# Key-key and query-key products of a DeltaNet layer: fp32 products of 128 columns against split products of 256 columns on shared stationary keys

## The chip, the core and the metric

The kernel runs on one core of a Trainium2 chip. The metric is the device time of one execution in microseconds (us); lower is better. Besides whole runs there is one profiled execution, whose trace gives each instruction's engine, start and duration. TensorE appears there as PE (matmuls) and PEld (loads of the stationary operand), VectorE as DVE, ScalarE as ACT, GpSimd as POOL, and the queue that issues all DMAs of this kernel as SP.

## What is computed

One layer of a diffusion backbone over 128 context and 2048 latent tokens (17 tiles of 128 tokens), in fp32: a modulated RMSNorm, an input projection, a convolution over three tokens with SiLU on queries, keys and values, a bidirectional gated DeltaNet beside a gated MLP, an output projection, and a feed-forward block. The change concerns the two matrices that the DeltaNet needs within each chunk:

```python
q = l2norm(q.reshape(B, T, H_A, DK)); k = l2norm(k.reshape(B, T, H_A, DK))
# per chunk, H_A = 4 heads of DK = 128 features
a_mat = where(strict, einsum('bnhcd,bnhsd->bnhcs', k_beta, k) * decay, 0.0)
qk = einsum('bnhcd,bnhsd->bnhcs', q, k) * decay
```

The kernel forms the raw products of keys with keys and of keys with queries per tile of 128 tokens and per head, and applies beta, decay and scale later. That is 17 x 4 = 68 tile-heads, two 128x128 products each.

## The kernel before

The work runs in phases. The first phase, which ends near 435 us of the profile, makes the projection of queries, keys and values, the convolution, and the products above, and writes all of them to DRAM scratch. Later phases (the scan over chunks, the gated MLP, the output projection, the feed-forward block) load them from there.

**Start.** Four half vectors of the modulation are computed first, by `mod_load` and `mod_sum`: eight loads of 128x512 weights each (`raw`, 256 KB) and eight fp32 matmuls that keep the two condition columns stationary and move 512 columns. I call them m0 to m3. Each result, a row of 2x512 named `first`, is transposed by `mod_out` into the scale `a1` or shift `b1`. Three tiles of x (`x`, 512 KB each) and ten border rows (`xh`) are loaded, normalized and transposed, and `column(k)` makes from them the two halves `kH` and `kL` of the k-th feature tile of the first block and stores them (`hH_d`, `hL_d`). m0 and m1 and the x tiles are all that column 0 needs; the later columns need m2 and m3 too.

**Split products.** A product of fp32 precision is formed by `mm3` from operands that are split into a rounded high part and a low remainder (type `fp32r`): high x high, high x low, low x high, three matmuls into one accumulator.

**Blocks.** Five blocks of three token tiles and one of two (`BLOCKS`) are worked one after the other. Per block there are twelve feature tiles (`feature_tile`: four heads each of keys, queries and values), each a projection of 24 matmuls of 386 to 388 columns (258 in the last block) into a bank of the pool `pj` (three banks), read by `convolve` on ACT and DVE. Four further steps of a tile are placed as side work between the projections of later tiles: `to_tokens` (transposes on PE, norms on ACT, results `kn` and `tk`), `to_features` (transposes back, copied by DVE to `kTt`, the keys with features on partitions), and `products`, once per block and head, 24 calls in all.

**Products before.** `products` makes, for each of two destinations `kk_d` and `qk_d`, one fp32 matmul of 128 columns per token tile, with a slice of `kTt` as stationary operand for the first destination and moving slices of `kTt` or of the query tile `x2` (line 625; on the chip each shows as two records). ACT copies each destination's bank of the pool `pt` (three banks) to `ev` (line 628), and SP stores it (line 629). `ev` shares four buffers, tag `tk`, with `kn` and `tk`.

**What sets the order.** A scheduler that works on the whole program puts the instructions of each engine into one fixed order; every engine and the SP queue then run that order strictly, waiting at an instruction until what it needs is there. Tiles come from pools whose buffers are handed out in turn; the pool `wp` has 49 buffers of 128x512 (`raw`, weights and their halves), and a load into a buffer waits for the last reader of what lay there.

Of the kernel before, what the change touches and what calls it, by code (L numbers as in the profile page):

```python
# [8 lines left out]
F32 = mybir.dt.float32  # L9
F32R = mybir.dt.float32r  # L10
# [3 lines left out]
ALU = mybir.AluOpType  # L14
# [3 lines left out]
P = 128  # L18
# [46 lines left out]
def hybrid_step(  # L65
# [7 lines left out]
    V, A, G, T = nc.vector, nc.scalar, nc.gpsimd, nc.tensor  # L73
    load = nc.sync.dma_start
    store = nc.sync.dma_start
# [10 lines left out]
    def f32(ap):  # L86
        return ap.bitcast(F32)
# [12 lines left out]
    kk_d = dp.tile([NT, P, H, P], F32, name="kk_d")  # L100
# [127 lines left out]
    def w512(name, dt=F32):  # L228
        return wp.tile([P, 512], dt, tag="w", name=name)
# [65 lines left out]
    with ExitStack() as ph:  # L295
# [52 lines left out]
        def mod_sum(raws, psum):  # L348

            pm = psum()  # L350
            for k in range(KT):
                T.matmul(pm[0:2, :], scond[:, k, :], raws[k], start=k == 0, stop=k == KT - 1)
            row = pf.tile([2, 512], F32, tag="first", name="first", bufs=2)
            A.copy(row, pm[0:2, :])
            return row

# [187 lines left out]
        def feature_tile(blk, bi, gi, h):  # L544

            hH, hL, ncol, segs = blk
            tiles = BLOCKS[bi]
            nt = len(tiles)
            n = nt * P
            c0 = tiles[0] * P  # L550
            j = gi * 4 + h
            u = {}

            def project(k):
                if k == 0:
                    u["ps"] = (pt if bi == 0 and j == 6 else pj)()
                wh, wl = W1[gi][k]
                mm3(u["ps"][:, :ncol], [(wh[:, h * P : (h + 1) * P], wl[:, h * P : (h + 1) * P],
                                         hH[k][:, :ncol], hL[k][:, :ncol])], first=k == 0, last=k == KT - 1)
                if k == KT - 1:  # L560
                    convolve()

            def convolve():
                ps = u["ps"]
                cv = pf.tile([P, 384], F32, tag="cv", name="cv", bufs=2)
                u["x2"] = x2 = pf.tile([P, 384], F32, tag="x2", name="x2", bufs=4)
                for s, o, m, _ in segs:
                    A.activation(cv[:, o : o + m], ps[:, s : s + m], AF.Copy, scale=convw[:, 1, j : j + 1])  # L568
                for s, o, m, _ in segs:
                    for w, sh in ((0, -1), (2, 1)):  # L570
                        V.scalar_tensor_tensor(out=cv[:, o : o + m], in0=ps[:, s + sh : s + sh + m],  # L571
                                               scalar=convw[:, w, j : j + 1], in1=cv[:, o : o + m],
                                               op0=ALU.mult, op1=ALU.add)
                A.activation(x2[:, :n], cv[:, :n], AF.Tanh, scale=0.5)
                V.scalar_tensor_tensor(out=x2[:, :n], in0=x2[:, :n], scalar=1.0, in1=cv[:, :n], op0=ALU.add,
                                       op1=ALU.mult)
                if gi == 0:
                    store(out=by_tiles(qT_d[:, :, h, :], slice(tiles[0], tiles[0] + nt)),
                          in_=x2[:, :n].rearrange("p (a d) -> p a d", d=P))

            def to_tokens():
                pq = pt()
                for i in range(nt):
                    T.transpose(pq[:, i * P : (i + 1) * P], u["x2"][:, i * P : (i + 1) * P], ident)  # L584
                rows = slice(c0, c0 + n)
                if gi == 2:
                    tk = pf.tile([P, 3, P], F32, tag="tk", name="tk", bufs=4)
                    A.copy(tk[:, :nt, :], pq[:, :n].rearrange("p (a b) -> p a b", b=P))
                    store(out=vt_d[rows, h * P : (h + 1) * P].rearrange("(a p) d -> p a d", p=P),
                          in_=tk[:, :nt, :])  # L590
                    return
                junk = p1.tile([P, P], F32, tag="junk2", name="junk2", bufs=1)
                if gi == 0:
                    for i, t in enumerate(tiles):
                        A.activation(junk, pq[:, i * P : (i + 1) * P], AF.Square,
                                     accum_out=ssq[:, t, h : h + 1])
                    return
                ss = smp.tile([P, 3], F32, tag="ss3", name="ss3")
                rk = smp.tile([P, 3], F32, tag="rk", name="rk")
                for i in range(nt):  # L600
                    A.activation(junk, pq[:, i * P : (i + 1) * P], AF.Square, accum_out=ss[:, i : i + 1])  # L601
                rsqrt_cols(rk[:, :nt], ss[:, :nt], nt, 1.0, 4 * EPS)
                u["kn"] = kn = pf.tile([P, 3, P], F32, tag="tk", name="kn", bufs=4)
                for i in range(nt):
                    A.activation(kn[:, i, :], pq[:, i * P : (i + 1) * P], AF.Copy, scale=rk[:, i : i + 1])
                store(out=kt_d[rows, h * P : (h + 1) * P].rearrange("(a p) d -> p a d", p=P),
                      in_=kn[:, :nt, :])

            def to_features():

                u["kTt"] = kTt = pf.tile([P, 384], F32, tag="kTt", name="kTt", bufs=3)
                pk = pt()
                for i in range(nt):
                    T.transpose(pk[:, i * P : (i + 1) * P], u["kn"][:, i, :], ident)
                V.tensor_copy(kTt[:, :n], pk[:, :n])
                store(out=by_tiles(kT_d[:, :, h, :], slice(tiles[0], tiles[0] + nt)),
                      in_=kTt[:, :n].rearrange("p (a d) -> p a d", d=P))

            def products(q):

                kTt = u["kTt"]
                for dst, rhs in ((kk_d, kTt), (qk_d, q["x2"])):
                    ps = pt()
                    for i in range(nt):
                        T.matmul(ps[:, i * P : (i + 1) * P], kTt[:, i * P : (i + 1) * P],  # L625
                                 rhs[:, i * P : (i + 1) * P], start=True, stop=True)
                    ev = pf.tile([P, 3, P], F32, tag="tk", name="ev", bufs=4)
                    A.copy(ev[:, :nt, :], ps[:, : nt * P].rearrange("p (a b) -> p a b", b=P))
                    store(out=dst[tiles[0] : tiles[0] + nt, :, h, :].rearrange("a p d -> p a d"),
                          in_=ev[:, :nt, :])  # L630

            u["main"] = [lambda k=k: project(k) for k in range(KT)]
            u["to_tokens"] = to_tokens
            u["to_features"], u["products"] = to_features, products
            return u
# [1435 lines left out]
```

## Time and profile before

| | |
|---|---|
| three runs | 2574.28, 2577.04, 2578.62 us, median 2577.04 us |
| profiled execution | 2580.59 us, its span 2578.7 us |
| PE busy in the span | 2539.4 us (98%), 15268 matmul records |
| DVE, ACT, POOL busy | 1836.7, 1259.7, 234.2 us (71%, 49%, 9%) |
| DMA | 588.66 MB, mean 228 GB/s |
| mean granted clock of TensorE | 0.997 |

The profile's page lists each engine's busy time over the span, then the span in slices, the DMA queues, the chain of work that ended last, and the costliest groups of instructions. A matmul's record lasts longer than the time for which it holds up the next one, since matmuls overlap in the pipeline: what a matmul costs in a full stream is the distance from its start to the next start. Some matmul records are missing from the later phases; in the first phase they are complete.

### The profile page before, as it was taken

The page shows a single profiled execution, that of the slowest core. Times are in us where ns is not written, and L with a number is a line of the kernel's source. Part 1 is how long each engine was busy: PE and PEld are TensorE (multiplying, and loading weights), DVE is VectorE, ACT ScalarE, POOL GpSimd, SP SyncE. Part 2 cuts the span into 40 slices and gives each one's busy share as a digit, 9 for nine tenths or more (in the row PEclk, how much of TensorE's full clock was granted, in tenths as well). Part 3 has the DMA queues.
Part 4 walks back from the last instruction along what each step waited for, and adds up shares of the span by engine and source line. Part 5 has one row for each costly group of instructions (what it writes and reads, how often), then busy time and mean ns, then how long its engine had stood idle before and what let it go on. Part 6 is the DMA issues. An engine that isn't in the chain of part 4 may idle for free.

```text
span 2578.7 us, 44496 instructions
## 1 busy us (share of the span) xinstructions
PE 2539.4 (98%) x15268; PEld 2139.2 (83%) x15268; DVE 1836.7 (71%) x3790; ACT 1259.7 (49%) x3119; POOL 234.2 (9%) x448
## 2 busy tenths in 40 slices
PE   9999999999999999999999999999999999999998
PEld 5999999788888787778888888888888888888887
DVE  5867757776677878886677876777675557685875
ACT  4755556555555667764355543544442433243442
POOL 3112212111111111210000000000000000000000
PEclk9999999999999999999999999999999999999999
DMA  8967737644454657885768789666579979786683
GB/s 293 307 209 216 209 111 256 225 158 153 145 156 159 214 165 243 277 274 176 281 204 257 231 270 358 194 181 188 148 248 370 331 273 330 259 259 205 221 264 113
DMA packets 503912, 588.66 MB, mean 228 GB/s; under 512 B 36148, under 2 KB 298588, under 8 KB 500102
## 3 DMA queue, kind: packets, MB, share of 16 engines
q1 hardware_dynamic: 503686, 585.82, 69.6%
q8 instruction: 120, 1.97, 0.3%
q14 instruction: 106, 0.87, 0.1%
HBM read 406.01 MB, written 179.67 MB: 227 GB/s over the span
## 4 chain that ended last, share of the span: by engine, by line
PE 89%; DMA 5%; DVE 4%; ACT 1%; issue 1%; POOL 0%; SPq 0%; POOLq 0%; DVEq 0%; ACTq 0%
PE f L241 17%; PE f L242 17%; PE f L243 17%; PE pj L241 7%; PE pj L243 7%; PE pj L242 7%; PE pd L1010 5%; PE pm L241 1%; PE pm L243 1%; PE pm L242 1%; DMA raw<-in_w_mod_dram 1%; PE pt L625 1%; PE pt L584 1%; PE pd L1093 1%; DMA hop_d<-opL 1%
## 5 line engine op out<-in xcount | busy, mean ns | idle before, releaser
L241 PE MATMUL f<-hop,zH 128*128 128x512 f32 (+1 forms) x976 | 376.2, 386 | 1.2 <-ACT zH L1531 1.2
L242 PE MATMUL f<-hop,zH 128*128 128x512 f32 (+1 forms) x976 | 376.1, 386 | 0.0
L243 PE MATMUL f<-hop,zL 128*128 128x512 f32 (+1 forms) x976 | 376.1, 386 | 0.0
L241 PE MATMUL f<-hop,wH 128*128 128x512 f32 x896 | 349.7, 391 | 0.6 <-ACT p L1604 0.6
L242 PE MATMUL f<-hop,wH 128*128 128x512 f32 x896 | 348.7, 389 | 0.0
L243 PE MATMUL f<-hop,wL 128*128 128x512 f32 x896 | 347.5, 389 | 0.0
L1531 ACT CAST zH<-zraw 128x512 fp32r<-128x512 f32 x240 | 146.9, 620 | 302.4 <-DMA zraw<-s_d 93.6
L241 PEld LDWEIGHTS f<-hop,zH 128*128 128x128 f32 x976 | 183.3, 188 | 38.6 <-ACT zH L1531 1.6
L243 PEld LDWEIGHTS f<-hop,zL 128*128 128x128 f32 x976 | 183.3, 188 | 37.3 <-DVE zL L1525 0.4
L242 PEld LDWEIGHTS f<-hop,zH 128*128 128x128 f32 x976 | 183.3, 188 | 36.9 <-issue 0.2
L1525 DVE TENSOR_TENSOR zL<-zraw,zH 128x512 fp32r<-128x512 f32 x240 | 163.2, 687 | 66.5 <-ACT zH L1531 54.0
L241 PEld LDWEIGHTS f<-hop,wH 128*128 128x128 f32 x896 | 168.2, 188 | 36.5 <-ACT p L1604 1.7
L243 PEld LDWEIGHTS f<-hop,wL 128*128 128x128 f32 x896 | 168.2, 188 | 35.3
L242 PEld LDWEIGHTS f<-hop,wH 128*128 128x128 f32 x896 | 168.3, 188 | 34.5
L241 PE MATMUL pj<-kH,wH 128*128 128x386 f32 (+2 forms) x568 | 190.5, 338 | 1.3 <-ACT junk L601 1.1
L243 PE MATMUL pj<-kH,wL 128*128 128x386 f32 (+2 forms) x568 | 189.7, 335 | 0.0
L242 PE MATMUL pj<-kL,wH 128*128 128x386 f32 (+2 forms) x568 | 189.5, 335 | 0.1
L184 POOL TENSOR_TENSOR r<-rsq,nhalf 128x1 f32<-128x1 f32 (+1 forms) x37 | 25.7, 694 | 1409.0 <-DVE rsq L183 1409.0
L571 DVE SCALAR_TENSOR_TENSOR cv<-pj,vec,cv 128x384 f32<-128x384 f32 (+2 forms) x164 | 87.0, 539 | 53.4 <-ACT cv L568 52.0
L1531 ACT CAST wH<-s 128x512 fp32r<-128x512 f32 x96 | 59.4, 621 | 124.6 <-DVE s L1525 118.3
L241 PEld LDWEIGHTS pj<-kH,wH 128*128 128x128 f32 x568 | 107.1, 189 | 4.4 <-issue 2.4
L202 DVE TENSOR_TENSOR wL<-raw,wH 128x512 fp32r<-128x512 f32 x120 | 81.7, 688 | 40.0 <-ACT wH L201 36.6
(418 smaller groups left out, 5806.9 us busy)
## 6 DMA issues: line engine op xcount, KB each, us to landing
zraw<-z_d SPq DMA_DIRECT2D x212, 256.0 KB
raw<-in_w_ff_dram SPq DMA_DIRECT2D x192, 256.0 KB
hop<-hop_d SPq DMA_DIRECT2D x28, 1024.0 KB
z_d<-c SPq DMA_DIRECT2D x96, 256.0 KB
zraw<-s_d SPq DMA_DIRECT2D x96, 256.0 KB
raw<-in_w_mod_dram SPq DMA_DIRECT2D x80, 256.0 KB
r<-in_w_ff_dram SPq DMA_DIRECT2D x80, 256.0 KB
s_d<-s SPq DMA_DIRECT2D x64, 256.0 KB
```

What stands on the lines that cost most here:

```text
L184: G.tensor_tensor(out=out, in0=t[:np_, :n], in1=nhalf[:np_, :n], op=ALU.pow)
L202: V.tensor_tensor(out=lo, in0=raw, in1=f32(h), op=ALU.subtract)
L241: T.matmul(ps, lh, rh, start=first and i == 0, stop=False, skip_group_check=more)
L242: T.matmul(ps, lh, rl, start=False, stop=False, skip_group_check=more)
L243: T.matmul(ps, ll, rh, start=False, stop=last and i == n - 1, skip_group_check=more)
L571: V.scalar_tensor_tensor(out=cv[:, o : o + m], in0=ps[:, s + sh : s + sh + m], scalar=convw[:, w, j : j + 1], in1=cv[:, o : o + m], op0=AL ...
L584: T.transpose(pq[:, i * P : (i + 1) * P], u["x2"][:, i * P : (i + 1) * P], ident)
L625: T.matmul(ps[:, i * P : (i + 1) * P], kTt[:, i * P : (i + 1) * P], rhs[:, i * P : (i + 1) * P], start=True, stop=True)
L1010: T.matmul(p[:, h, :], lhs[:, h, :], rhs[:, h, :], start=True, stop=True)
L1093: T.matmul(py[:, h], u["X"][:, h, :], pm[:, h], start=True, stop=True)
L1525: V.tensor_tensor(out=out, in0=a, in1=b, op=op)
L1531: A.copy(h, src)
```

## The change

`products` is written anew. ACT rounds keys and queries into one tile `kqH` (high parts, keys in half 0 and queries in half 1), DVE subtracts to get `kqL` (low parts). For each token tile three matmuls follow, as in `mm3`, and each moves keys and queries of the tile together, 2 x 128 = 256 columns, on the stationary keys. A bank of `pt` takes two token tiles, so a call needs two banks for three tiles; ACT copies the first with 512 and the second with 256 columns per partition into `ev`, which now holds both destinations, and SP stores the two halves. `kqH`, `kqL` and `ev` have one buffer each (`kqH` takes over the space of `xh`). To make room, the shared buffers of tag `tk` go from four to three, and the rows `first` move from a pool of their own (two buffers) into `wp`.

```diff
-            row = pf.tile([2, 512], F32, tag="first", name="first", bufs=2)
+            row = w512("first")[0:2, :]
...
-                    tk = pf.tile([P, 3, P], F32, tag="tk", name="tk", bufs=4)
+                    tk = pf.tile([P, 3, P], F32, tag="tk", name="tk", bufs=3)
...
-                kTt = u["kTt"]
-                for dst, rhs in ((kk_d, kTt), (qk_d, q["x2"])):
+                hi = pf.tile([P, 2, 384], F32R, tag="xh", name="kqH", bufs=1)
+                lo = pf.tile([P, 2, 384], F32R, tag="kqL", name="kqL", bufs=1)
+                for w, x in enumerate((u["kTt"], q["x2"])):
+                    A.copy(hi[:, w, :n], x[:, :n])
+                    V.tensor_tensor(out=lo[:, w, :n], in0=x[:, :n], in1=f32(hi)[:, w, :n], op=ALU.subtract)
+                ev = pf.tile([P, 2, 3, P], F32, tag="ev", name="ev", bufs=1)
+                for i0 in range(0, nt, 2):
+                    m = min(2, nt - i0)
                     ps = pt()
-                    for i in range(nt):
-                        T.matmul(ps[:, i * P : (i + 1) * P], kTt[:, i * P : (i + 1) * P],
-                                 rhs[:, i * P : (i + 1) * P], start=True, stop=True)
-                    ev = pf.tile([P, 3, P], F32, tag="tk", name="ev", bufs=4)
-                    A.copy(ev[:, :nt, :], ps[:, : nt * P].rearrange("p (a b) -> p a b", b=P))
-                    store(out=dst[tiles[0] : tiles[0] + nt, :, h, :].rearrange("a p d -> p a d"),
-                          in_=ev[:, :nt, :])
+                    for i in range(m):
+                        c = slice((i0 + i) * P, (i0 + i + 1) * P)
+                        out = ps[:, i * 256 : i * 256 + 256].rearrange("p (w d) -> p w d", w=2)
+                        for j, (st_, mv) in enumerate(((hi, hi), (hi, lo), (lo, hi))):
+                            T.matmul(out, st_[:, 0, c], mv[:, :, c], start=j == 0, stop=j == 2)
+                    A.copy(ev[:, :, i0 : i0 + m, :].rearrange("p w a d -> p a w d"),
+                           ps[:, : m * 256].rearrange("p (a w d) -> p a w d", a=m, w=2))
+                for w, dst in enumerate((kk_d, qk_d)):
+                    store(out=dst[tiles[0] : tiles[0] + nt, :, h, :].rearrange("a p d -> p a d"), in_=ev[:, w, :nt, :])
```

In the changed program lines 624 (`kqH`), 625 (`kqL`), 634 (matmuls), 635 (copies to `ev`) and 638 (stores) take the place of 625, 628 and 629. Over the kernel the counts move so: 136 fp32 matmuls of 128 columns go, 204 split matmuls of 256 columns come; 48 copies on ACT go and 44 come, with 48 roundings; 48 subtractions on DVE come; the 48 stores stay. Nothing else changes in number.

The scheduler gives all engines another order in the first phase. Past it, the order of every engine is that of before, apart from buffer numbers and line numbers (on PE the last 14775 of 17290 instructions).

The SP queue at the start of the program, before, from the eleventh load on (`raw` from `w_mod` with eight or sixteen loads are m0 to m3; line 377 loads weights of a fifth, later part of the modulation; 747, 670 and 671 load small constants):

```order
L190 DMA raw<-in_w_mod_dram 128x512 x16
L411 DMA xh<-in_x_sample_dram 2x1024 x5
L424 DMA x<-in_x_prompt_dram 128x1024
L424 DMA x<-in_x_sample_dram 128x1024 x2
L190 DMA raw<-in_w_mod_dram 128x512 x8
L190 DMA raw<-in_w_in_dram 128x512 x4
L772 DMA abr<-in_w_ab_dram 128x128
L377 DMA raw<-in_w_mod_dram 128x512 x2
```

m0 and two rows of small constants stand ahead; so m0, m1 and m2 come first, then x, then m3 and the first four projection weights. The same place in the changed program:

```order
L190 DMA raw<-in_w_mod_dram 128x512 x8
L411 DMA xh<-in_x_sample_dram 2x1024 x5
L424 DMA x<-in_x_prompt_dram 128x1024
L424 DMA x<-in_x_sample_dram 128x1024 x2
L780 DMA abr<-in_w_ab_dram 128x128
L377 DMA raw<-in_w_mod_dram 128x512 x2
L390 DMA mrow<-in_b_mod_dram 2x512
L755 DMA wsT<-in_w_spatialT_dram 128x512
L678 DMA alog<-in_a_log_dram 128x8
L679 DMA dtb<-in_dt_bias_dram 128x8
L190 DMA raw<-in_w_mod_dram 128x512 x8
L377 DMA raw<-in_w_mod_dram 128x512 x2
```

m2 now stands behind x and seven other loads. What follows there:

```order
L534 DMA hH_d<-kH 128x128
L534 DMA hL_d<-kL 128x128
L534 DMA hH_d<-kH 128x2x128
L534 DMA hL_d<-kL 128x2x128
L190 DMA raw<-in_w_mod_dram 128x512 x8
L190 DMA raw<-in_w_in_dram 128x512 x20
```

m3 and the projection weights have moved behind the four stores of column 0, which wait for DVE.

ACT in the fourth block (token tiles 9 to 11), before, around two calls of `products` (568 and 574 belong to `convolve`, 528 to `column`, 588 to `to_tokens`):

```order
L628 COPY ev<-pt 128x384 x2
L568 ACTIVATE cv<-pj,vec 128x384
L588 COPY tk<-pt 128x384
L628 COPY ev<-pt 128x384 x2
L574 ACTIVATE x_4012<-cv 128x384
```

Each call has two copies there. The same engine and block in the changed program:

```order
L635 COPY ev<-pt 128x2x2x128
L635 COPY ev<-pt 128x2x128
L624 CAST kqH<-kTt 128x384
L624 CAST kqH<-x_3958 128x384
L574 ACTIVATE x_4211<-cv 128x384
L568 ACTIVATE cv<-pj,vec 128x384
L528 ACTIVATE kH<-full,b_197 128x384 x2
L588 COPY tk<-pt 128x384
L635 COPY ev<-pt 128x2x2x128
L635 COPY ev<-pt 128x2x128
```

Behind the two copies of one call now stand the two roundings of the next call, and the next copies into the single `ev` wait for the stores of the call before.

PE at another call of the same block (the second of its four), in the changed program:

```order
L634 MATMUL pt<-kqH 128x256 x2
L241 MATMUL pj<-kH,wH 128x386
L242 MATMUL pj<-kL,wH 128x386
L243 MATMUL pj<-kH,wL 128x386
L241 MATMUL pj<-kH,wH 128x386
L634 MATMUL pt<-kqL,kqH 128x256
L634 MATMUL pt<-kqH,kqL 128x256
L634 MATMUL pt<-kqH 128x256
L634 MATMUL pt<-kqL,kqH 128x256
```

Two high x high products go ahead, four projection matmuls stand between, and the products with low parts follow, where before the fp32 matmuls of a destination stood together.

More of the change, by code (lines that the diff above doesn't have):

```diff
@@ L602, in to_tokens @@
                 rsqrt_cols(rk[:, :nt], ss[:, :nt], nt, 1.0, 4 * EPS)
-                u["kn"] = kn = pf.tile([P, 3, P], F32, tag="tk", name="kn", bufs=4)
+                u["kn"] = kn = pf.tile([P, 3, P], F32, tag="tk", name="kn", bufs=3)
                 for i in range(nt):
```

## The prediction

> **What bounds the kernel now.** I read the page first: the busy times and the chain that ended last.
>
> ```profile
> span 2578.7 us, 44496 instructions
> PE 2539.4 (98%) x15268; PEld 2139.2 (83%) x15268; DVE 1836.7 (71%) x3790; ACT 1259.7 (49%) x3119; POOL 234.2 (9%) x448
> PE 89%; DMA 5%; DVE 4%; ACT 1%; issue 1%; POOL 0%; SPq 0%; POOLq 0%; DVEq 0%; ACTq 0%
> ```
>
> PE carries 89% of the chain. Next the windows of the first phase (columns: PE, PEld, DVE, ACT, POOL busy, granted clock, DMA share, GB/s):
>
> ```profile
> 0.00:50.00 50.00, 47.81 (x186) 22.83 (x187) 24.80 (x97) 21.73 (x42) 23.81 (x104) 1.00 0.93 323
> 60.00:440.00 380.00, 377.18 (x2448) 363.66 (x2447) 265.07 (x573) 222.14 (x682) 73.71 (x174) 1.00 0.71 213
> ```
>
> From 60 to 440 us PE is busy for 99%, DVE for 70%, ACT for 58%. So there a shorter PE stream shortens the run, and work on the other two is free while no matmul waits for it. In the first 50 us the DMA share is 0.93: the start is near a bound by loads.
>
> **The products on PE.** The line's groups and one call, instruction by instruction:
>
> ```profile
> L625 PE MATMUL pt<-kTt x136: 270/275/377, 92.0 to 427.8; 128*128 128x128 f32 x136
> L625 PE MATMUL pt<-x,kTt x136: 270/275/276, 93.8 to 429.4; 128*128 128x128 f32 x136
> ...
> 154.31 0.34 PE L242 MATMUL pj<-kL,wH 128*128 128x386 f32 x1
> 154.49 0.83 PE L625 MATMUL pt<-kTt 128*128 128x128 f32 x6
> 155.07 0.43 PE L243 MATMUL pj<-kH,wL 128*128 128x386 f32 x1
> 155.34 0.34 PE L241 MATMUL pj<-kH,wH 128*128 128x386 f32 x1
> 155.51 0.34 PE L242 MATMUL pj<-kL,wH 128*128 128x386 f32 x1
> ```
>
> A matmul of 386 columns lasts 0.34 us but is followed after 0.17 to 0.18. The six records of one destination take from 154.49 to 155.07, 0.58 us, and the projection matmul behind them holds 0.27 instead of 0.18: together 0.67. Twenty calls of three tiles have two such groups (26.8 us), four calls of two tiles have two thirds of that (3.6): 30.4 us in all.
>
> The new matmuls are 204 of 256 columns. Nearest in size are those of the gates:
>
> ```profile
> 385.34 0.28 PE L646 MATMUL pj<-kL,abW 128*128 128x258 f32 x1
> 385.46 0.28 PE L645 MATMUL pj<-kH,abW 128*128 128x258 f32 x1
> 385.58 0.28 PE L646 MATMUL pj<-kL,abW 128*128 128x258 f32 x1
> ```
>
> They start 0.12 apart: 204 x 0.12 = 24.5. Lower bound: per column as at 386 (0.175 / 386 x 256 = 0.116), 23.7. Upper bound: the whole 0.175 of the 386-column matmul, 35.7, which would turn the gain into a loss of 5.3; the moving operand here is two strips of 128 columns, which no row shows, but at 258 columns the row is nearest and I take it. **Term A: 24.5 - 30.4 = -5.9.** So the product of two split triples on shared keys is not three times cheaper, only a fifth.
>
> **What ACT and DVE get.** Groups by shape, from 60 to 440 us (count, busy, mean ns, idle before):
>
> ```profile
> L201 ACT CAST wH<-raw 128x512 fp32r<-128x512 f32 x33 | 20.1, 641 | 7.4 <-DMA raw<-in_w_in_dram 4.2 <-DMA raw<-in_w_mod_dram 3.2
> L628 ACT COPY ev<-pt 128x384 f32<-128x384 f32 x40 | 18.7, 481 | 15.5 <-PE pt L625 14.4 <-DMA kk_d<-ev 0.8 <-DMA qk_d<-ev 0.2
> L628 ACT COPY ev<-pt 128x256 f32<-128x256 f32 x8 | 2.9, 372 | 0.5 <-PE pt L625 0.4
> L202 DVE TENSOR_TENSOR wL<-raw,wH 128x512 fp32r<-128x512 f32 x32 | 21.3, 681 | 4.0 <-ACT wH L201 3.6 <-PE pj L243 0.3
> ```
>
> A copy grows by 109 ns per 128 columns (481 - 372). So a rounding of 384 columns is about 641 - 109 = 530 ns and one of 256 columns 420: 40 x 0.53 + 8 x 0.42 = 24.6 us more on ACT. The subtraction, scaled likewise, is about 0.57 and 0.46: 26.5 us more on DVE. Copies: 0.59 + 0.37 instead of 2 x 0.48, no change. Over 380 us ACT goes from 58 to 65%, DVE from 70 to 77%. Both stay under PE: nothing, as long as their order does not hold up `convolve`, whose banks of `pj` PE needs. If that cover were gone, a call's 1.1 us on ACT times 24 would be 26 us; the idle of 15.5 us before the copies shows that ACT waits for PE there, not the reverse.
>
> **The single buffers.** A call's first copy into `ev` now waits until both stores of the call before have landed; behind it in ACT's order stand the roundings of the next call and `convolve`. Before, such waits were rare and short:
>
> ```profile
> 118.26 0.36 SPq L629 DMA_DIRECT2D kk_d<-ev  x1
> 122.53 0.38 SPq L629 DMA_DIRECT2D kk_d<-ev  x1
> 122.78 0.48 ACT L628 COPY ev<-pt 128x384 f32<-128x384 f32 x1 [0.79 <-DMA kk_d<-ev]
> 126.39 0.48 ACT L588 COPY tk<-pt 128x384 f32<-128x384 f32 x1 [0.95 <-DMA kk_d<-ev]
> ```
>
> A store takes 3.9 to 4.5 us from its issue until its reader's buffer is free. The loop of a call is then: copies 0.59 + 0.37, two issues of about 0.4 each, landing 3.9 to 4.5: 5.7 to 6.3. By the changed order 28 to 30 projection matmuls stand between two calls of a block, so PE needs 29 x 0.175 + 9 x 0.12 = 6.2 us per call. The two are level: ACT will wait a little, PE has three banks each of `pt` and `pj` in between. **Term B: +1.5,** bounds 0 and +5 (18 calls that follow another in the same block, 0.3 us each).
>
> **The start.** m2 is moved behind x and seven other loads on SP, m3 behind the stores of column 0, which wait for DVE.
>
> ```profile
> 10.00:16.00 6.00, 6.00 (x15) 1.06 (x13) 0.29 (x2) 0.58 (x1) 4.73 (x12) 1.00 1.05 392
> ...
> 11.67 4.46 PE L352 MATMUL pj<-raw,scond 128*2 128x512 f32 x10
> 16.39 7.89 PE L352 MATMUL pj<-raw,scond 128*2 128x512 f32 x18
> 28.11 1.02 PE L352 MATMUL pm<-raw,scond 128*2 128x512 f32 x2 [0.84 <-DMA raw<-in_w_mod_dram]
> 32.67 3.59 PE L352 MATMUL pm<-raw,scond 128*2 128x512 f32 x8
> 36.20 0.62 PE L241 MATMUL pj<-kH,wH 128*128 128x388 f32 x2
> ...
> 25.28 1.06 ACT L335 ACTIVATE junk<-x 128x1024 bf16<-128x1024 f32 x1 [0.98 <-DMA x<-in_x_sample_dram]
> 27.38 1.06 ACT L335 ACTIVATE junk<-x 128x1024 bf16<-128x1024 f32 x1 [0.95 <-DMA x<-in_x_sample_dram]
> ```
>
> Loads run at 392 GB/s, so 262 KB take 0.67 us; a matmul of L352 is two records of 0.43, 0.86 us. m1's 16 records are the ten at 11.67 and six of the eighteen at 16.39, so m1 ends at 16.39 + 6 x 0.43 = 19.0, as before. PE went straight on with m2 there. Now x comes first: its third tile, at 27.4 before, eight loads earlier, 27.4 - 8 x 0.67 = 22.0. Then 3.25 loads' worth (two of line 377, `wsT`, `abr` of a quarter) and m2's first: 22.0 + 4.25 x 0.67, about 25. Thus PE has little but transposes from 19 to 25. m2 needs 8 x 0.86 = 6.9 from there: 32. The transposes of the third x stand behind m2's first two matmuls, near 27; then ACT, DVE, and the stores near 29; m3's loads, issued behind them, land from about 33 (a landing takes about 4 us, above), and m3 lasts until 40; with the small matmuls behind it, the first L241 comes near 42, of which 1.3 us were work that before stood behind 36.2 (at 36.8 to 39.5). That is 40.9 against 36.2: **term C: +5.** Lower bound, by the bytes alone: behind the third x stand 3.25 loads, m2's 8, two of line 377, column 0's stores (384 KB, 1.5) and m3's 8, so m3's last lands at 22.0 + 22.75 x 0.67 = 37.2, its matmul ends at 38.1, +1.9; upper bound +8, if PE also runs at half clock for a while or the later columns, which need m2 and m3, come late as well. Hidden behind PE's backlog it is not, since all PE work up to the first L241 is short of loads.
>
> **A wait near 70 us** may shrink by this:
>
> ```profile
> 65.03 1.06 ACT L467 ACTIVATE junk<-x 128x1024 bf16<-128x1024 f32 x1 [5.00 <-DMA x<-in_x_sample_dram]
> 70.96 0.52 PE L584 MATMUL pt<-ident,x 128*128 128x128 f32 x3 [0.44 <-DVE x L575]
> 72.61 0.41 PE L241 MATMUL pj<-kH,wH 128*128 128x388 f32 x1 [1.13 <-ACT junk L601]
> ```
>
> ACT stood 5 us for the second block's x, and PE lost 1.13 + 0.44 there and some 0.7 beside, 2.3 in all. With PE 5 us later and x later by less, part of this goes: **term D: -1,** bounds -2.3 and +1 (x as late as PE).
>
> **Sum:** -5.9 + 1.5 + 5 - 1 = -0.4. Past the first phase nothing moves. The profiled execution is the span 2578.7 and 1.9 around it, 2580.6, which is 3.6 above the median of the runs; so 2580.2 for it and 2576.6 in terms of the median. By the bounds the sum lies between -5.9 + 0 + 1.9 - 2.3 = -6.3 and -5.9 + 5 + 8 + 1 = +8.1: 2570.7 to 2585.1.
>
> **The clock.** PE idle costs more than its length when it is followed by a lower clock:
>
> ```profile
> PE pd L1010 <- DMA S<-in_state_delta_dram: 1.9, 1, 1.9
> ...
> 500.00:510.00 10.00, 8.54 (x55) 7.28 (x55) 3.55 (x10) 4.53 (x13) 0.00 (x0) 0.83 0.28 83
> ```
>
> PE waited 1.9 us there for a state, and in these 10 us the granted clock was 0.83: 10 x 0.17 = 1.7 us lost, as half speed for 3.4 us would. In the new start PE stands from 19 to 25 with little to do. The Trainium skill, "TensorE: Matmul & The Clock Gate", Part 1, states that the array falls to half its clock after an idle window of about 3.4 us and returns after as long a stretch of work; the row above agrees in size, and by that rule the sum would be -0.4 + 1.7 = +1.3, still within the noise. I keep it inside the upper bound of term C, since a load that is late hides slow matmuls.
>
> **Rivals.** First, *the start costs nothing in the end*: the lost time is work that PE had ahead of its loads, and the second block's x, the weights' halves and the wait at 70 us catch up. For it speaks the 2.3 us lost near 70 to loads that don't move as far as PE; against it the first L241, which cannot come before m3. Then -5.9 - 2.3 + 1.5 = -6.7, about 2570. Second, *the start costs the upper bound*: PE's pause brings the half clock, and the columns 1 to 7, each released by m2 and m3, arrive one by one behind 20 weight loads; for it speaks the DMA share of 0.93; -5.9 + 1.5 + 8 = +3.6, and with the wait near 70 us staying or growing +1, +4.6, up to 2584. Third, slower by one mechanism, *the single `ev` sets PE's pace*: it decides once the loop of a call is longer than PE's 6.2 us, that is, once a store lands later than about 4.4 us after its issue; at 5 us, 18 x 0.6 = 11 us instead of 1.5, so +9, 2586. The landings of 3.9 to 4.5 speak for a near thing, three banks of `pt` against it. Fourth, that the strips run slower than 0.12: at 0.175 2588; little speaks for it.
>
> **Chances.** Terms about as taken, within 0.2% (5 us, about what a measurement of this kernel can tell from no change): 0.55, its own range 2572 to 2582. First rival 0.19, second 0.14, third 0.09, fourth 0.03. Faster by over 0.2%: 0.19; slower: 0.26. The range of 2570 to 2585 takes in the first rival and most of the second.
>
> **What the profile after would show.** Term A: 256-column matmuls 0.12 apart and no slowed follower. Term B: ACT's copies into `ev` with idle behind `kk_d` or `qk_d`, PE's waits for `pt` or `pj` under 0.3 us a call. Term C: the first L241 near 41 to 44, PE waits for `raw` of `w_mod` before 33. Term D: the waits at 70 us smaller. ACT and DVE about 25 us busier. I am wrong if the first L241 stays at 36 to 38 or passes 46, if the matmuls stand 0.15 or more apart, or if PE waits for ACT at most calls.

## The result, and the profile after

The changed kernel is slower: 2588.43 us median of 6 runs (2583.85 to 2590.84) against 2577.2 us, median of 6 runs of before (2574.28 to 2578.62), a ratio of 1.0043 with the 95% interval 1.003 to 1.0056, or +11 us. Forecast was no change, 2576.6, with 2570 to 2585 as the range. The profiled execution took 2585.38 us, 3 under its median, that of before 3.4 over its own: the two traces show 5 of the 11 us.

The page's first rows, and the windows that answer to those of before:

```profile
span 2583.7 us, 44419 instructions
PE 2537.8 (98%) x15200; PEld 2134.2 (83%) x15200; DVE 1858.5 (72%) x3838; ACT 1273.5 (49%) x3163; POOL 235.6 (9%) x448
...
0.00:50.00 50.00, 43.28 (x140) 15.68 (x141) 17.88 (x76) 14.52 (x28) 20.18 (x104) 0.93 0.84 284
60.00:440.00 380.00, 375.54 (x2403) 362.07 (x2402) 290.01 (x622) 238.62 (x726) 77.44 (x174) 1.00 0.70 211
```

The first 50 us lost 4.5 us of PE's busy time (47.81 to 43.28) and 7% of the clock. From 60 to 440 us PE is still busy for 99%; DVE did 25 us and ACT 16 us more in that window.

**The products on PE** came as forecast. A call in the third block:

```profile
250.52 0.40 PE L634 MATMUL pt<-kqH 128*128 128x256 f32 x2
250.76 0.34 PE L241 MATMUL pj<-kH,wH 128*128 128x386 f32 x1
250.93 0.34 PE L242 MATMUL pj<-kL,wH 128*128 128x386 f32 x1
251.11 0.28 PE L634 MATMUL pt<-kqL,kqH 128*128 128x256 f32 x1
251.22 0.28 PE L634 MATMUL pt<-kqH,kqL 128*128 128x256 f32 x1
251.34 0.28 PE L634 MATMUL pt<-kqH 128*128 128x256 f32 x1
```

They start 0.12 apart and slow no follower; all 204 sum to 25.0 us (from each one's start to the next) where the fp32 products took 30.5, the slowed follower of each group included.

**The start**, on PE:

```profile
21.35 0.33 PE L514 MATMUL pt<-ident,x 128*128 128x128 f32 x1 [0.82 <-DVE x L337]
22.91 0.58 PE L361 MATMUL pm<-ident,first 2*128 2x2 f32 x4 [1.23 <-ACT first L354]
24.05 0.47 PE L514 MATMUL pt<-ident,x 128*128 128x128 f32 x1 [0.56 <-DVE x L337]
25.67 3.58 PE L352 MATMUL pj<-raw,scond 128*2 128x512 f32 x4 [1.14 <-DMA raw<-in_w_mod_dram]
29.18 0.48 PE L514 MATMUL pt<-ident,x 128*128 128x128 f32 x1
29.58 5.31 PE L352 MATMUL pj<-raw,scond 128*2 128x512 f32 x12
35.40 1.02 PE L352 MATMUL pm<-raw,scond 128*2 128x512 f32 x2 [0.51 <-DMA raw<-in_w_mod_dram]
36.70 6.56 PE L352 MATMUL pm<-raw,scond 128*2 128x512 f32 x14
45.29 0.34 PE L241 MATMUL pj<-kH,wH 128*128 128x388 f32 x1
```

PE waits four times between 20 and 26 us. The first four records of m2 then take 3.58 us; four of m2 took 1.88 before:

```profile
24.54 1.88 PE L352 MATMUL pj<-raw,scond 128*2 128x512 f32 x4
```

PE runs at half speed there; the granted clock from 25.67 to 29.20 us is 0.50. The first L241 starts at 45.29 instead of 36.20.

**The end of the first phase** was not in the forecast. SP's last store of products and its first loads of hidden tiles `hH` for the next phase, before and after, and PE's wait for them:

```profile
431.99 0.42 SPq L629 DMA_DIRECT2D qk_d<-ev  x1
443.25 0.79 SPq L1238 DMA_DIRECT2D hH<-hH_d  x2
```

```profile
441.26 0.51 SPq L638 DMA_DIRECT2D qk_d<-ev  x1
450.93 0.90 SPq L1246 DMA_DIRECT2D hH<-hH_d  x2
...
PE pm L241 <- DMA hH<-hH_d: 4.1, 1, 4.1
...
450.00:500.00 50.00, 45.39 (x314) 34.37 (x313) 37.82 (x99) 26.79 (x67) 13.49 (x17) 0.93 0.75 264
```

The last matmul of PE's projections starts 4.4 us later than before (430.40 against 426.01), but the last product store is 9.3 us later and the loads behind it on SP 7.7. PE stands 4.1 us for them and then works for a while at a low clock (0.93 over 50 us, that is 3.5 us lost; 1.00 before).

To compare kernels across stages I use one mark in the next phase, eight small matmuls that every kernel has, at 551.50 in before and 558.13 after:

```profile
551.50 1.06 PE L1276 MATMUL pm<-vg,wsT 128*128 128x128 f32 x8
```

```profile
558.13 1.06 PE L1284 MATMUL pm<-vg,wsT 128*128 128x128 f32 x8
```

From the mark to the end of the span before takes 2027.2 us, after 2025.6, and a second trace of the changed kernel 2029.8: the stages behind it vary by some us from one execution to the next, in the same order. Four kernels below have two traces each; their marks differ by 0.2 to 3.1 us, the stretches behind by 0.5 to 6.2. What a kernel gained or lost before the mark is the steadier number of a single trace. One caution: the single trace of before has, ahead of its mark, a wait of 1.9 us for a state near 500 us and a low clock behind it (quoted with the prediction), which the others show in part or not at all, so a loss read at the mark may be too small by up to 3.6 us.

At the mark the changed kernel is 6.6 us late, and its trace accounts for that. 9.1 are there at the first L241, 1.4 of them small matmuls pulled ahead (43.92 to 45.29 us). The products save 5.5, and PE's waits from there to its last projection are 4.7 instead of 2.6: together 4.3, and the last projection is 4.4 late. The other 2.2 come behind it: the wait for `hH` and its low clock in place of the shorter waits of before.

### The profile page after: what moved, and what is told of

Same layout as the page of the kernel before. It is cut to its first block, busy times and chain, and to the rows that moved or that the text cites. A ratio compares the mean times of both kernels' runs of the same rounds, so it can differ in the third digit from the quotient of the medians.

```text
span 2583.7 us, 44419 instructions
## 1 busy us (share of the span) xinstructions
PE 2537.8 (98%) x15200; PEld 2134.2 (83%) x15200; DVE 1858.5 (72%) x3838; ACT 1273.5 (49%) x3163; POOL 235.6 (9%) x448
## 5 line engine op out<-in xcount | busy, mean ns | idle before, releaser
L241 PE MATMUL f<-hop,zH 128*128 128x512 f32 (+1 forms) x976 | 376.2, 386 | 1.2 <-ACT zH L1539 1.2
L241 PE MATMUL f<-hop,wH 128*128 128x512 f32 x896 | 349.6, 391 | 2.6 <-ACT p L1612 1.8
L241 PEld LDWEIGHTS f<-hop,zH 128*128 128x128 f32 x976 | 183.4, 188 | 38.6 <-ACT zH L1539 1.6
L241 PEld LDWEIGHTS f<-hop,wH 128*128 128x128 f32 x896 | 168.2, 188 | 38.5 <-ACT p L1612 2.9
L241 PE MATMUL pj<-kH,wH 128*128 128x386 f32 (+2 forms) x568 | 190.3, 337 | 2.4 <-DVE cv L571 1.3
L241 PEld LDWEIGHTS pj<-kH,wH 128*128 128x128 f32 x568 | 107.0, 189 | 5.5 <-DVE cv L571 1.6
L242 PEld LDWEIGHTS pj<-kL,wH 128*128 128x128 f32 x568 | 107.4, 189 | 1.1 <-issue 0.4
```

The lines of the kernel that those rows point to most:

```text
L241: T.matmul(ps, lh, rh, start=first and i == 0, stop=False, skip_group_check=more)
L242: T.matmul(ps, lh, rl, start=False, stop=False, skip_group_check=more)
```

## The experiments

Two theories. **S**: the late start costs the time, the products are a gain. **P**: the new work on ACT and DVE costs it, by where it stands in orders that ACT and SP follow strictly. All ratios are to runs of before on the same chip (medians 2577.2 us for the first row of the changed kernel, 2578.9 to 2580.5 for the others); intervals are 95%. A mark comes from one traced execution.

| kernel | ratio | first L241 | mark |
|---|---|---|---|
| before | | 36.20 | 551.50 |
| changed; again | 1.0043; 1.0045 | 45.29; 45.00 | 558.13; 558.36 |
| rows moved alone | 1.0056 | 45.95 | 563.84 |
| rows apart; again | 1.0019; 1.0027 | 36.18; 36.37 | 552.02; 550.33 |
| m2 first | 1.0034 | 42.58 | 558.46 |
| `ev` in pairs | 1.0014 | 37.22 | 552.60 |
| unread work | 1.0024 | 37.12 | 557.58 |
| last block fp32 | 1.0005 | 36.16 | 547.96 |
| the same, `ev` in pairs | 1.0019 | 37.03 | 557.79 |
| middle blocks; again | 0.9986; 0.9990 | 36.20; 36.29 | 548.03; 551.08 |
| unread work, middle blocks | 1.0008 | 36.60 | 552.22 |
| first and last fp32; again | 0.9990; 0.9980 | 36.59; 36.98 | 543.17; 542.86 |
| gaps filled | 1.0045 | 46.56 | 560.03 |

**Rows moved alone.** The kernel before with one line:

```diff
-            row = pf.tile([2, 512], F32, tag="first", name="first", bufs=2)
+            row = w512("first")[0:2, :]
```

> The kernel before with one line changed: the modulation rows `first` lie in the pool wp, as in the changed kernel; products stay fp32. Theory S (the start is what cost the time): the first L241 near 45 us as in the changed kernel (36.2 before), PE's clock below 1 before 50 us, about +6.5 us left at 550 us, so 2583 to 2586 against 2577. Theory P (the new products' work and waits cost it, the start is absorbed later): within 3 us of before, although the first L241 is late.

2593.68 us, 1.0056 (1.0043 to 1.007): +14, as much as the whole change or more (the intervals overlap), and more than either theory expected. SP's order at the start is that of the changed kernel, and so is PE's picture:

```profile
25.70 3.57 PE L352 MATMUL pj<-raw,scond 128*2 128x512 f32 x4 [1.58 <-DMA raw<-in_w_mod_dram]
36.46 1.02 PE L352 MATMUL pm<-raw,scond 128*2 128x512 f32 x2 [0.82 <-DMA raw<-in_w_mod_dram]
45.95 0.34 PE L241 MATMUL pj<-kH,wH 128*128 128x388 f32 x1
```

So one line about where a row of 2x512 lies makes the late start. Nothing of it is caught up in this trace, which is of the slowest of the six runs (2600.61): 9.75 us at the first L241 are 12.3 at the mark.

**Rows apart.** The changed kernel with the rows in two buffers that are idle at the start:

```diff
+        FN = []
...
-            row = w512("first")[0:2, :]
+            row = pf.tile([P, 2, 384], F32, tag=("ev", "kqL")[len(FN) % 2], name="first", bufs=1).rearrange("p a b -> p (a b)")[0:2, 0:512]
+            FN.append(1)
```

> The changed kernel with the rows `first` taken out of wp and laid into the buffers of `ev` and `kqL` in turn; by the order SP starts as before (m0, m1, m2, x, m3). Theory S: the first L241 back at 36 to 37 us, -5.5 us from the products, up to +4 from the late last product call at the end of the first phase: 2573 to 2578. Theory P: as slow as the changed kernel, 2585 or more.

2586.41 us, 1.0019 (1.0009 to 1.0028). The start is back (36.18) but the kernel is still 5 us slower than before, although PE's products are 5.5 us shorter. S is not the whole: some 10 us are lost elsewhere. The trace is of the fastest of the twelve runs (2581.5) and shows 6 of them ahead of the mark, which is 0.5 late with 5.5 saved; two places stand out. At the first block's third call:

```profile
101.66 0.97 SPq L462 DMA_DIRECT2D x<-in_x_sample_dram  x2
110.98 0.94 PE L625 MATMUL pt<-kTt 128*128 128x128 f32 x6 [0.81 <-ACT junk L595]
```

```profile
105.92 0.70 SPq L465 DMA_DIRECT2D x<-in_x_sample_dram  x1
111.88 0.41 PE L241 MATMUL pj<-kH,wH 128*128 128x386 f32 x1 [0.77 <-ACT kH L531]
112.27 1.06 ACT L470 ACTIVATE junk<-x 128x1024 bf16<-128x1024 f32 x1 [0.28 <-DMA x<-in_x_sample_dram]
114.13 0.38 PE L637 MATMUL pt<-kqH 128*128 128x256 f32 x1 [1.83 <-ACT junk L598]
114.74 0.42 PE L637 MATMUL pt<-kqH 128*128 128x256 f32 x1
114.96 0.41 PE L637 MATMUL pt<-kqL,kqH 128*128 128x256 f32 x1
```

The first fence is before, the second rows apart. The third x tile of a later block (before, the second of the two issues at 101.66) is issued about 4 us later on SP; ACT, which must square that tile first, reads PE's bank late; PE stands 1.83 instead of 0.81 us, and then its 256-column matmuls start 0.21 apart, half speed (granted clock 0.93 from 100 to 125 us, 1.00 before: 1.75 us). The other place is the end of the phase, with the 4.1 us for `hH` again.

**m2 first.** In the changed kernel the line that loads m2 moves ahead of the sums that make the first rows:

```diff
+        m2 = mod_load(1, 0)
         r0 = mod_sum(m0, pm1)
         r1 = mod_sum(m1, pj)
-        m2 = mod_load(1, 0)
```

> The changed kernel with only the line that allocates and loads m2 moved ahead of the sums of m0 and m1; `first` stays in wp. By the order m2's eight loads stand ahead of x again, m3's eight still behind the small loads but ahead of column 0's stores. Theory S (m2 and m3 loaded late, because wp's buffers are handed out in turn and m2's come after `first`): the first L241 at 37 to 40 us, 2575 to 2581. If the place of `first` itself costs (its copy, its buffer), the time stays at 2585 or more.

2587.73 us, 1.0034 (1.0021 to 1.0048), 7 us or more above what theory S expected; first L241 at 42.58, later than expected. SP's order has m2 ahead of x again, m3 still late. This fits a reading of how the one line works: buffers of `wp` are handed out in the program's turn, so a load whose buffer comes after that of `first` is not ordered ahead of the sum that fills `first`. With m2 in front again 2.7 of the 9.1 us return; m3 keeps the rest.

**`ev` in pairs.** The changed kernel, start restored, `ev` as two tiles of tag `tk` with five buffers, copied one by one:

```diff
...
-                ev = pf.tile([P, 2, 3, P], F32, tag="ev", name="ev", bufs=1)
+                evs = [pf.tile([P, 3, P], F32, tag="tk", name="ev", bufs=5) for _ in range(2)]
...
```

> The changed kernel with `first` in the buffer of `kqL` (start as before) and `ev` as two tiles of the shared tag `tk`, which has five buffers, so that a call's copies need not wait for the stores of the call before; two copies per bank instead of one. If the single `ev` costs time, 2 to 5 us faster than the kernel with rows apart and fewer waits of ACT for kk_d and qk_d; if it doesn't (theory S), equal within 2 us.

2583.31 us, 1.0014 (1.0004 to 1.0023), against 1.0019 (1.0009 to 1.0028): by the ratios 1.3 us faster, by the medians 3.1. The intervals overlap, and the runs alone would allow either expectation. In the changed kernel itself, what ended ACT's idle time ahead of the first copies into `ev` reads:

```profile
L635 ACT COPY ev<-pt 128x512 f32<-128x512 f32 x24 | 14.0, 581 | 13.9 <-PE pt L634 10.9 <-DMA hH_d<-kH 2.1 <-PE pj L242 0.7
```

It is PE; 2.1 us are put down to a store, of another tile, and only 0.2 us of all of ACT's waits from 60 to 445 us to a store of `ev`. So waits for the single buffer are not where the time goes; that it costs a us or two in some other way is not excluded.

**Unread work.** The kernel before, start as before, fp32 products, and ahead of each call the roundings and subtractions, read by nobody (`first` lies in the buffer of `kqL`):

```diff
...
+                for w, x in enumerate((kTt, q["x2"])):
+                    A.copy(hi[:, w, :n], x[:, :n])
+                    V.tensor_tensor(out=lo[:, w, :n], in0=x[:, :n], in1=f32(hi)[:, w, :n], op=ALU.subtract)
```

> The kernel before (fp32 products) with the 48 roundings on ACT and 48 subtractions on DVE added in front of each call, read by nobody; `tk` with four buffers, `first` in the buffer of `kqL`; SP starts as before. PE's stream stays as in the kernel before, so only what the added work and its place in the orders cost is seen. Theory W (the added work on ACT and DVE and the places in their orders eat the products' gain): +6 to +11 us against before, PE waiting near 111 us and at the end of the first phase. Theory C (it is the longer chain of a call, rounding, subtraction, copy, single buffers, that costs): within 3 us of before, since no matmul needs the added results.

2586.24 us, 1.0024 (1.0011 to 1.0036): +6 us for work that no matmul waits for, and 6.1 at the mark. PE's waits in its trace:

```profile
71.42 0.52 PE L584 MATMUL pt<-ident,x 128*128 128x128 f32 x3 [1.61 <-DVE ab L661]
73.55 0.52 PE L584 MATMUL pt<-ident,x 128*128 128x128 f32 x3 [0.74 <-DVE x L575]
115.50 0.94 PE L630 MATMUL pt<-kTt 128*128 128x128 f32 x6 [1.24 <-ACT junk L595]
129.63 0.41 PE L241 MATMUL pj<-kH,wH 128*128 128x386 f32 x1 [0.73 <-DVE cv L571]
...
PE pm L241 <- DMA hH<-hH_d: 1.7, 1, 1.7
```

The waits near 70 and 111 us are longer than before, those at 129 us and for `hH` are new, and the clock is 0.93 from 75 to 100 and from 450 to 475 us. 0.9 of the 6.1 stand at the first L241 already. P holds, as the expectation's theory W: the work is not hidden in the first blocks and at the end of the phase, although from 60 to 440 us ACT is idle for 38% of the time and DVE for 25%. The scheduler orders everything anew with this work too; whether the work's time costs or the order that comes with it, these runs don't tell apart.

**Last block fp32**, twice. Rows apart, and in the last block the old products:

```diff
+                if bi == len(BLOCKS) - 1:
+                    for dst, rhs in ((kk_d, kTt), (qk_d, q["x2"])):
...
+                    return
```

> The kernel with rows apart, but the products of the last block (four calls of two tiles) as before in fp32; by the order the last product stores and the loads of hH behind them stand as in the kernel before. If the late last call makes PE wait 4 us for hH at the end of the first phase: that wait falls to about 1 us, PE's clock there is back at 1, 3 to 5 us faster than rows apart, that is at the time of before or 1 to 2 us under it. If the wait has another cause: unchanged at 2586, +0.7 for the four fp32 calls.

2581.7 us, 1.0005 (0.9995 to 1.0014), mark 547.96; 4.7 us under rows apart, as expected, and level with before. PE no longer waits for `hH` (its waits there are 1.5 us for `hL` and 1.5 for a state), and the last product store is at 430.87, the loads of `hH` at 441.29, as in before.

> The same with `ev` as pairs of the shared tag `tk` (five buffers). Its last product stores stand later in SP's order than in the kernel with the last block in fp32 and `ev` single. If SP's order at the end of the phase decides: 1 to 3 us slower than that one; if the work on ACT and DVE decides: equal to it.

2583.41 us, 1.0019 (1.0007 to 1.003), mark 557.79. By its trace PE waited 1.4 and 4.1 us around 115 us with this form of `ev`, a place that neither expectation named, so it tells nothing of SP's order; the intervals of the two overlap.

**Middle blocks**, in two sets of runs: split products in the third to fifth block, fp32 in the others.

> The kernel with rows apart and split products in the third, fourth and fifth block only (twelve calls of three tiles), fp32 in the first, second and last. PE saves 12 x 0.26 = 3.1 us there, and the places at which PE waited more than before (near 111 us and at the end of the phase) have the fp32 products again. Theory C or W alike: 2 to 3 us faster than before. If it isn't faster than before, the loss is spread over all calls or is the order's alone.

2575.87 us, 0.9986 (0.9975 to 0.9997): 3.6 us faster by the ratio, a little more than expected.

> Rows apart, split products in the third to fifth block, once more: 2 to 5 us faster than before (0.9986 in the first set).

2577.22 us, 0.9990 (0.9981 to 1.0000): 2.6 us, the low end of what was expected, with an interval that reaches no change.

**Unread work, middle blocks only.**

> The kernel before with the unread roundings and subtractions in the third, fourth and fifth block only (24 and 24 of 48 and 48). If the added work costs only where ACT and SP are tied to loads (the first blocks and the last): equal to before within 2 us, where all 48 cost 6. If it costs by its amount: half of that, 3 us.

2581.44 us, 1.0008 (0.9999 to 1.0017), and 0.7 us late at the mark. The runs lie between the two expectations and settle nothing between 0 and half; the trace leans to nothing. So that the added work is free in the middle blocks rests on the kernels that split products there, not on this run.

**The changed kernel and rows apart, again, on one chip.**

> The changed kernel itself, beside the kernel with rows apart on one chip, so that the start's price is read within one set of runs: by the two sets so far (1.0043 and 1.0019 of before) 5 to 7 us slower than rows apart. A second trace shows whether the first L241 near 45 us, the low clock before 50 us and the wait for hH near 452 us are there again.

2589.88 us, 1.0045 (1.0031 to 1.0058), five runs. First L241 at 45.00, and again

```profile
25.00:50.00 25.00, 22.70 (x75) 8.31 (x76) 10.98 (x45) 6.77 (x15) 10.39 (x44) 0.93 0.83 283
...
PE pm L241 <- DMA hH<-hH_d: 4.5, 1, 4.5
```

> The kernel with rows apart once more: again 4 to 6 us slower than before (its earlier profiled execution was the fastest of its runs, 5 us under their median). The trace should show in one of the known places (68 to 75 us, 111 to 115, 446 to 460, the scan) what most of its runs have and that one had not.

2585.38 us, 1.0027 (1.0018 to 1.0037), a little more than the 4 to 6 us expected. On this chip the start costs 4.5 us of run time, less than the 5 to 7 expected; by the two traces of each, 6.1 to 8.0 at the mark. Near 114 PE waited 2.44 us this time, for `hH` only 1.8, and the mark is at 550.33, not later; what made this execution longer than the other trace of the kernel (2584.2 against 2579.7) lies behind the mark, 2033.9 against 2027.7. What does that there is open.

**First and last block fp32**, in two sets: the line of the last block with `bi in (0, len(BLOCKS) - 1)`, so that 16 calls are split.

> Rows apart, split products in the second to the fifth block (16 calls of three tiles), fp32 in the first and last. The first block's calls lie at 94 to 124 us, where ACT waits for the second and third block's x; the second block's at 159 to 187, where PE was busy throughout. If only the first and the last block's places cost: 16 x 0.26 = 4.2 us off PE, 1 us faster than the kernel with three split blocks, 4 to 5 under before. If every call outside the middle costs: slower than that one.

2578.26 us, 0.9990 (0.9981 to 0.9999), mark 543.17: 2.6 us by the ratio and 0.6 by the medians, less than the 4 to 5 expected. Its trace is 8.3 ahead at the mark and loses 7.1 behind it (2034.3 against 2027.2).

> Rows apart, fp32 in the first and last block, once more, beside the kernel with three split blocks on one chip: by PE's stream 1 us faster than that one; its first trace was 8 us ahead of before at 550 us, its runs only 0.1% ahead. If that trace was typical of the first phase: again 7 to 9 us ahead at 550 us.

2574.66 us, 0.9980 (0.9971 to 0.9989): 5 us faster than before, the lowest ratio here; whether it beats the middle blocks alone, the overlapping intervals leave open. Its trace is 8.6 us ahead at the mark:

```profile
542.86 1.06 PE L1299 MATMUL pm<-vg,wsT 128*128 128x128 f32 x8
```

5.4 of that stand at PE's last projection (420.57 against 426.01), some 4 of them from the 16 calls by the prices above; the rest is mostly the wait for a state near 500 us with its low clock, which the trace of before has (quoted with the prediction) and this one has not.

**Gaps filled.** The changed kernel with one unread fp32 matmul behind each x tile of the first block:

```diff
+        fill = pt()
         for x in xs0:
             norm_rows(x)
+            T.matmul(fill[:, 0:512], ident, x[:, 0:512], start=True, stop=True)
```

> The changed kernel with one fp32 matmul of 512 columns (0.86 us, result unread) added on PE behind each normalized x tile of the first block, so that PE's pauses from 20 to 26 us are partly filled; loads and their order stay. If the clock falls because PE pauses: PE's clock stays near 1 in the first 50 us, m2's records start 0.43 apart instead of 0.85, and the first L241 comes 1 to 3 us earlier than 45. If the late loads of m3 alone set the end of the start: the clock is repaired but the first L241 stays at 44.5 or later. If the clock has nothing to do with the pauses: clock 0.93 again, and 2 to 3 us later for the added work.

2591.39 us, 1.0045 (1.0029 to 1.0061). The clock was 0.97 and 0.90 in the two windows of 25 us, and the second and third of the added matmuls (two records each) themselves ran at half speed, 2.08 us where the first took 1.12:

```profile
21.81 1.12 PE L429 MATMUL pt<-x,ident 128*128 128x512 f32 x2 [1.29 <-DVE x L337]
23.93 2.08 PE L429 MATMUL pt<-x,ident 128*128 128x512 f32 x2 [0.55 <-DVE x L337]
46.56 0.34 PE L241 MATMUL pj<-kH,wH 128*128 128x388 f32 x1
```

PE still stood 1.29 us before the first of them. The gaps were not filled well enough to keep the clock, so this run doesn't say what a start at full clock would cost.

## Why the prediction was wrong

- **Term A, the products on PE (-5.9): right.** Measured -5.5, from the 258-column row that it was taken from.
- **The added work on ACT and DVE (nothing): the step that failed most.** Its size was right: a rounding of 384 columns took 519 ns (530 forecast), a subtraction 550 to 554 (570). The cover was wrong. I took shares over 380 us, 58% and 70%; the unread work cost 6 us. By the traces, it stands in strict orders in front of instructions that PE or SP wait for, in stretches that are tied to loads: the first block (x tiles) and the end of the phase (the last product stores, with the next phase's loads behind them on SP).
- **"Past the first phase nothing moves": wrong in what mattered.** The order is the same there, but SP's loads come when the last product store has been issued, 9.3 us later than before. The wait for `hH` went from none to 4.1 and 4.5 us, and a low clock follows it. Leaving the last block in fp32 took the wait away.
- **Term C, the start (+5): the order right, the lateness too small.** m2's first load was forecast for 25 us and PE waited until 25.67, m3's for 33 and it was 35.40. The first L241 was forecast for 42 and came at 45.29; without the work pulled ahead that is 7.7 us late, not 4.7. In the first trace the granted clock of 0.96 and 0.91 over two windows of 25 us is 25 x 0.13 = 3.3 us of lost clock:

```profile
0.00:25.00 25.00, 20.45 (x66) 7.74 (x66) 6.18 (x31) 8.06 (x14) 9.82 (x60) 0.96 0.81 285
25.00:50.00 25.00, 22.83 (x74) 7.94 (x75) 11.70 (x47) 6.46 (x14) 10.36 (x44) 0.91 0.86 283
```

  and 1.75 in the second (1.00 and 0.93). Part of it fell where PE had nothing to do; the first four records of m2 lost 1.7. The prediction weighed +1.7 for this and left it out, on the ground that late loads hide slow matmuls. Here slow matmuls made a load late: behind those four records in PE's order stands the transpose of the third x tile (29.18), DVE needs it for column 0, SP issues column 0's stores from 30.49 and only behind them, from 32.36, m3's loads. The Trainium skill, "TensorE: Matmul & The Clock Gate", Part 1, says that the array drops to half its clock after an idle window of about 3.4 us; the trace agrees in the drop, but it came with PE's four pauses of 0.56 to 1.23 us among small transposes in place of one long one. In run time the start cost 4.5 us beside the new products, near the +5, and 14 alone.
- **Term D, the wait near 70 us (-1): wrong sign.** The place moved to 77 to 86 us and cost 3.0 us in excess starts instead of 2.3.
- **Term B, the single buffers (+1.5): not seen.** ACT's waits for them come to 0.2 us, at most 2.3 with the store of another tile, and pairs of buffers made no difference clear of the noise.
- **The second rival** (the start at its upper bound) came nearest in its mechanism, but its sum still counted the products' work as hidden. Its own +4.6 also gives 2581.6 in terms of the median; the 2584 it states is in terms of the profiled execution. The 2586 and 2588 of the third and fourth rivals are nearer to the measured time by luck: `ev` set no pace, and the matmuls stood 0.12 apart.

Up to the mark, the forecast of -0.4 became +6.6: 0.4 more from term A, 2.7 from term C, 1.6 from waits in the blocks (+2.1, where B and D together were +0.5), 2.2 from the end of the phase.

By whole runs, rows apart are +5 to +7 on two chips, so 10 to 12 us are lost there beside the 5.5 that PE saves; the start adds 4.5 on the one chip where both ran. The unread work accounts for 6 of the 10 to 12. No run isolates the rest: the longer chain of a call and what lies behind the mark are candidates, and its cause stays open. The terms don't add in every order: the start alone, without the new products, cost 14. One reason that the traces show is that the pause near 111 us in rows apart is short in the changed kernel (0.37 and 0.94 us near 120), whose PE is late by then.

## What to carry to other kernels

Do not count work on an engine with idle time as free where that engine itself waits in a strict order for a load; take its cover from each stretch, not from the mean of a phase, and look above all at the first blocks and at the last stores ahead of the next phase's loads. A small tile that moves into a pool whose buffers go round can hold back the later loads of that pool: compare the order of the queue before and after, and give such a tile a buffer that is idle at that time. A rewrite that gains in the middle and loses at the edges can be kept for the middle alone, here 0.998 to 0.999 instead of 1.0043.

## What the runs showed of the hardware

PE's clock fell without one long pause. Near 111 us in rows apart two pauses of 0.77 and 1.83 us with one matmul between them were followed by matmuls 0.21 us apart instead of 0.12; at the start, pauses of about 1 us with transposes between them did the same, and three matmuls of 512 columns added among them did not prevent it (0.97 and 0.90). So 2.6 us of waits cost 4.4 (1.75 by the clock, above).
